# The order of the last three products of a down projection, and the width of its closing layer norm

## The chip, the cores and the metric

The kernel runs on one core of one Trainium2 chip. A time is device microseconds of one execution, from start to end; lower is better. The engines of a core work side by side, each through its own queue in order: PE (matrix multiply), DVE (elementwise and statistics), ACT (casts and activation functions), POOL and SP, which here mostly issue transfers. PE writes its results to banks of a small accumulator memory, from which DVE and ACT read them.

## The reference

The reference is one layer of a hybrid decoder on 1024 positions of 1024 columns in float32: layer norm, a gated mix of a convolution branch and a state-space branch, a projection, a layer norm, then a gated feed-forward block with a causal convolution, and a last layer norm. What the change touches is the end of it:

```python
def conv_ffn(h, w_up, dw_w, dw_b, w_down):
    u = causal_dwconv(h @ w_up, dw_w, dw_b)
    gate, val = jnp.split(u, 2, axis=-1)
    return (jax.nn.silu(gate) * val) @ w_down
...
        ffn = conv_ffn(h, w_ffn_up[l], ffn_dw_w[l], ffn_dw_b[l], w_ffn_down[l])
        h = layer_norm(DN_ALPHA * h + ffn, ln2_g[l], ln2_b[l])
```

The down projection multiplies 1024 x 2816 activations by a 2816 x 1024 weight matrix; the result is added to the residual rows times 2 to the power 1/4, and each row is normalised, scaled and shifted.

## The kernel before

**Precision.** Each float32 operand is split into a high part (a cast by ACT, L1192) and a low part (the operand minus the high part, by DVE, L1193). A block product is three matmuls: high by high (L180), high by low (L181), low by high (L182).

**The down projection** (`down`) is computed by a scheme of Strassen's kind. Rows, columns and the inner dimension are halved, and seven products of sums of quarters replace eight plain ones. The tuple `products` gives their order. A product has 11 steps (`k`); a step multiplies one 128-deep slice into four banks, one for each row tile of 128 rows by 512 columns, so a product has 11 x 4 x 3 = 132 matmuls. There are two sets of four banks: X (`acc` in the profile) and Y (`sm`). A product marked `True` starts its banks anew; one marked `False` adds to what is in them, which is how the sums of products are formed. The function named third in each entry runs for each row tile when the product is complete: DVE adds the bank to the rows (`own`, L1210, with the residual's factor; `more`, L1213, without) or subtracts it. Product numbers in the code run from 0; the text counts from the first to the seventh.

**Rows.** `rows` holds the eight output tiles (rs[0] to rs[7]) of 128 rows, each with an early half E and a late half L of 512 columns. The residual reaches them from memory by `load_rows`, on POOL's queue: one small copy, then four transfers of 256 KB. Row tiles 0 to 3 are complete after `four`, row tiles 4 to 7 after `three`. Each of these two takes the statistics of its half (L224) and calls `ln_out` for the tile: aggregate of the statistics (L238), square root on ACT (L239), reciprocal (L240), then the normalisation in two passes over the columns (L244: subtract the mean, times g; L247: times the reciprocal, plus b), and the store by SP.

**Loading.** `load` prepares one step: SP loads the activation slice, and a weight quarter or two, to tiles `dr` and `do` of 1024 columns that come from two pools of three; DVE adds two quarters where the product wants a sum (L1122); ACT casts; DVE subtracts. The result is a tile `w_dn`, from two pools of three that take turns, so a step's tile comes free when PE is done with the step six before. The last four steps of the last product have a tile of their own (`last`). In the fifth product (`five`) the weight is the sum of `a21` and `a22`: two weight loads and an addition for each step. In the sixth (`four`) it is `a22`: one load, no addition. In the seventh (`three`) it stands ready in `c4`.

**What sets the order.** The order on each engine is a scheduler's, which works from the order of the code and the priorities in it: loads have a high one (L1147), `ln_out` of tile 7 has a raised one, the other tiles' `ln_out` have none. In the seventh product the last eight steps run bank by bank, so that the banks are completed 24 matmuls apart; in the others all four banks are completed in the last step.

Of the kernel before, what the change touches and what calls it, by code (L numbers as in the profile page):

```python
# [17 lines left out]
D = 1024  # L18
T = 1024
HALF = 512  # L20
# [34 lines left out]
def kernel(  # L55
# [15 lines left out]
    V, A, G, TE, SY = nc.vector, nc.scalar, nc.gpsimd, nc.tensor, nc.sync  # L71
# [1013 lines left out]
    def down(upp, dp):  # L1085

        LAST, EARLY = 8, 5
        X, Y = [bank(1) for _ in range(4)], [bank(0) for _ in range(4)]  # L1090

        def flat_big(name):
            return big_tile(name).bitcast(F32).rearrange("p i k t -> p (i k t)")

        kept, rows = flat_big("c3"), flat_big("rows")
        c3 = [kept[:, k * HALF : (k + 1) * HALF] for k in range(NK)]
        c4 = [dp.tile([P, HALF], F32, name=f"c4_{k}") for k in range(NK - 1)]
        c4.append(upp.tile([P, HALF], F32, tag="s3", name="c4_last"))
        rs = [rows[:, t * D : (t + 1) * D] for t in range(8)]
        sts = [dp.tile([P, 2, 6], F32, name=f"st_f{t}") for t in range(8)]  # L1100

        E, L = slice(0, HALF), slice(HALF, D)
        gb = []

        def load_rows(p, w):
            t0, cs = {0: (0, E), 1: (0, L), 2: (4, L), 4: (4, E)}[p]
            G.tensor_copy(
                rows.rearrange("p (t n) -> p t n", n=D)[:, t0 : t0 + 4, cs.start : cs.start + 1],
                w[:, 0, :4].bitcast(F32).unsqueeze(2),
            )  # L1110
            for t in range(t0, t0 + 4):
                G.dma_start(rs[t][:, cs], h1_scr[t * P : (t + 1) * P, cs])
            if p == 2:
                dp.tile([P, 32], F32, name="down_pad")
                for n, start in (("g", RW_2G), ("b", RW_2B)):
                    r = upp.tile([P, D], F32, tag="o", bufs=3, name=f"ln2_{n}")
                    G.dma_start(r, prow[start : start + D].partition_broadcast(P))
                    gb.append(r)


        def add(dst, x, y):
            V.tensor_tensor(out=dst, in0=x, in1=y, op=ALU.add)  # L1122

        n_steps, n_raw = 0, 0

        def raw(name):
            nonlocal n_raw
            n_raw += 1
            pl, tag = ((wst, "st"), (upp, "raw"))[n_raw % 2]
            return pl.tile([P, D], F32, tag=tag, bufs=3, name=f"{name}_{n_raw}")  # L1130

        last = []

        def load(p, k):

            nonlocal n_steps
            a11, a21, a12, a22 = (wdown[h * NK + k, :, cs] for h in range(2) for cs in (E, L))
            x = (
                b11_scr[k],
                b2_scr[k][:, E],  # L1140
                t32_scr[k][:, L],
                t32_scr[k][:, E],
                t41_scr[k][:, L],
                t41_scr[k][:, E],
                b2_scr[k][:, L],
            )[p]
            with tc.high_priority(offset=4000):  # L1147
                st = raw("dr")
                w_st = st[:, E]
                SY.dma_start(st[:, L], x)  # L1150
                if p == 0 and k < EARLY:
                    SY.dma_start(w_st, a11)
                    G.tensor_copy(c3[k], w_st)
                elif p == 0:
                    w_st = c3[k]
                    SY.dma_start(w_st, a11)
                elif p == 1:
                    w_st = c4[k]
                    SY.dma_start(w_st, a12)
                elif p == 2:  # L1160
                    other = raw("do")[:, E]
                    SY.dma_start(other, a21)
                    SY.dma_start(w_st, a22)
                    add(c3[k], c3[k], other)
                    add(w_st, w_st, c3[k])
                    add(c4[k], c4[k], w_st)
                elif p == 3:
                    w_st = c3[k]
                elif p == 4:
                    other = raw("do")[:, E]  # L1170
                    SY.dma_start(w_st, a21)
                    SY.dma_start(other, a22)
                    add(w_st, w_st, other)
                elif p == 5:
                    SY.dma_start(w_st, a22)
                else:
                    w_st = c4[k]
                if p == 6 and k >= NK - 4:
                    if not last:
                        last.append(big_tile("last").rearrange("p i k t -> p (i k t)"))  # L1180
                    w = last[0][:, (k - NK + 4) * 2 * D : (k - NK + 5) * 2 * D]
                    w = w.rearrange("p (i n) -> p i n", i=2)
                else:
                    own = n_steps % 2 and n_steps > 2
                    w = (dp if own else wsp).tile(
                        [P, 2, D], F32R, tag="w", bufs=3, name=f"w_dn{p}_{k}"
                    )
                cuts = ((slice(0, D), st),) if w_st is not c3[k] and w_st is not c4[k] else (
                    (E, w_st), (L, st[:, L])
                )  # L1190
                for cs, src in cuts:
                    A.copy(w[:, 0, cs], src)  # L1192
                    V.tensor_tensor(  # L1193
                        out=w[:, 1, cs], in0=src, in1=w[:, 0, cs].bitcast(F32), op=ALU.subtract
                    )
            n_steps += 1
            return w

        def block(ps, w, t, first, k):
            mm3(  # L1200
                ps,
                lambda i: w[:, i, HALF + t * P : HALF + (t + 1) * P],
                lambda i: w[:, i, :HALF],
                first and k == 0,
                k == NK - 1,
                not first,
            )

        def own(ps, r, cs, op):
            V.scalar_tensor_tensor(out=r[:, cs], in0=r[:, cs], scalar=ALPHA, in1=ps, op0=ALU.mult, op1=op)  # L1210

        def more(ps, r, cs, op):
            V.tensor_tensor(out=r[:, cs], in0=r[:, cs], in1=ps, op=op)  # L1213

        def one(t):
            own(X[t], rs[t], E, ALU.add)

        def two(t):
            more(Y[t], rs[t], E, ALU.add)
            ln_part(dp, rs[t], sts[t], 0)  # L1220

        def six(t):
            own(X[t], rs[t], L, ALU.subtract)

        def seven(t):
            own(Y[t], rs[4 + t], L, ALU.add)

        def five(t):
            more(X[t], rs[4 + t], L, ALU.subtract)
            ln_part(dp, rs[4 + t], sts[4 + t], 1)  # L1230

        def four(t):
            more(Y[t], rs[t], L, ALU.add)
            ln_part(dp, rs[t], sts[t], 1)
            ln_out(dp, t, rs[t], *gb, sts[t])

        def three(t):
            own(X[t], rs[4 + t], E, ALU.add)
            ln_part(dp, rs[4 + t], sts[4 + t], 0)
            ln_out(dp, 4 + t, rs[4 + t], *gb, sts[4 + t])  # L1240

        products = (
            (X, True, one),
            (Y, True, two),
            (X, False, six),
            (Y, True, seven),
            (X, False, five),
            (Y, False, four),
            (X, False, three),
        )  # L1250
        for p, (banks, first, then) in enumerate(products):
            end = NK - LAST if p == 6 else NK
            for k in range(end):
                w = load(p, k)
                for t in range(4):
                    block(banks[t], w, t, first, k)
                if k == 4 and p in (0, 1, 2, 4):
                    load_rows(p, w)
            ws = {k: load(p, k) for k in range(end, NK)}
            for t in range(4):  # L1260
                for k in ws:
                    block(banks[t], ws[k], t, first, k)
                then(t)

    def ln_out(own, t, r, g, b, st):

        with tc.high_priority(offset=200 if t == 7 else 0):
            mv, rstd = ln_stats(own, [r], f"f{t}", [st])
            halves = [slice(q * HALF, (q + 1) * HALF) for q in range(2)]
            for cs in halves:  # L1270
                ln_apply(r[:, cs], mv, rstd, 0, g[:, cs], b[:, cs])
                SY.dma_start(out[t * P : (t + 1) * P, cs], r[:, cs])

# [143 lines left out]
```

## Time and profile before

| what | value |
|---|---|
| time, median of 3 runs | 1951.15 us (1951.04 to 1954.07) |
| the profiled execution, first to last instruction | 1951.6 us |
| PE busy | 1926.3 us (99%) |
| DVE busy | 1633.5 us (84%) |
| ACT busy | 1105.9 us (57%) |
| POOL busy | 133.7 us (7%) |
| fifth, sixth and seventh product start at | 1852.06, 1881.98 and 1911.90 us |
| last matmul ends at | 1941.98 us |

The profile's own execution has no time beside its span; the span is 0.45 us above the median of the runs. PE is the busiest engine. A row of the timeline reads: start, duration, engine, line of the code, operation, the tile written and the tiles read, size, and in brackets how long the engine had stood idle and what ended that. An instruction's duration is a little longer than the distance to the next one on a full engine, since the two overlap.

### The profile page before, as it was taken

To read this page: it belongs to the slowest core of one execution; us is meant where nothing else is said; L and a number is where in the kernel's file an instruction comes from. 1 tells how busy PE (TensorE), PEld (TensorE's weight loads), DVE (VectorE), ACT (ScalarE), POOL (GpSimd) and SP (SyncE) were. 2 spreads that over 40 slices of the span, in tenths; PEclk is the share of its full clock that TensorE was granted. 3 is DMA by queue.
4 is the path that set the end of the run, shared out by engine and by line. 5 is a ranking of instruction groups with operands and counts; after the bars stand their busy time and mean duration, and the time that the engine had idled before them with its cause. 6 is when DMAs were issued, how large, how long until landed. Compare 5 with 4: busy or idle time off the path is not lost.

```text
span 1951.6 us, 24929 instructions
## 1 busy us (share of the span) xinstructions
PE 1926.3 (99%) x9128; PEld 1575.7 (81%) x9128; DVE 1633.5 (84%) x2215; ACT 1105.9 (57%) x1841; POOL 133.7 (7%) x184
## 2 busy tenths in 40 slices
PE   7999999999999999999999999999999999999998
PEld 6888888887888887888888888888888888888886
DVE  7799999997666889999999956588998887878778
ACT  6767777664453367877765545365655454453442
POOL 0100000000400010000000040001000000011000
PEclk9999999999999999999999999999999999999999
DMA  6434343534546542424353454576443332368572
GB/s 223 132 114 130 108 136 118 177 100 141 178 128 215 207 131 96 143 104 136 107 174 108 139 180 129 159 267 243 156 157 108 113 103 90 113 230 268 180 253 108
DMA packets 104011, 297.68 MB, mean 153 GB/s; under 512 B 12432, under 2 KB 12464, under 8 KB 103888
## 3 DMA queue, kind: packets, MB, share of 16 engines
q1 hardware_dynamic: 87840, 244.68, 37.5%
q0 software_dynamic: 13744, 47.21, 7.8%
q10 hardware_dynamic: 2304, 4.20, 0.6%
q8 instruction: 71, 1.16, 0.3%
q14 instruction: 52, 0.43, 0.1%
HBM read 246.22 MB, written 49.82 MB: 152 GB/s over the span
## 4 chain that ended last, share of the span: by engine, by line
PE 78%; issue 11%; DVE 5%; DMA 3%; ACT 2%; POOL 1%; SPq 0%; DVEq 0%; ACTq 0%; POOLq 0%
PE acc L181 21%; PE acc L180 21%; PE acc L182 21%; PE sm L180 3%; PE sm L182 3%; PE sm L181 3%; PE sm L642 2%; PE sm L628 1%; PE sm L632 1%; DMA do<-wdown 1%; PE sm L593 1%; PE acc L333 1%; DMA m<-cum_scr 1%; DVE w_dn L1193 1%; DVE rows L244 1%
## 5 line engine op out<-in xcount | busy, mean ns | idle before, releaser
L545 DVE SCALAR_TENSOR_TENSOR c<-v,pc,c 128x512 f32<-128x512 f32 x480 | 346.1, 749 | 6.8 <-ACT c L534 5.6
L180 PE MATMUL acc<-hT,w_c 128*128 128x512 f32 x368 | 147.2, 400 | 0.0
L181 PE MATMUL acc<-hT,w_c 128*128 128x512 f32 x368 | 146.9, 399 | 0.0
L182 PE MATMUL acc<-hT,w_c 128*128 128x512 f32 x368 | 144.9, 394 | 0.0
L607 ACT ACTIVATE m<-m,cums 128x128 f32<-128x128 f32 x256 | 79.0, 398 | 64.5 <-DMA m<-cum_scr 60.7
L1052 DVE SCALAR_TENSOR_TENSOR fo<-u,pc,fo 128x1024 f32<-128x1024 f32 x88 | 111.3, 1289 | 0.0
L500 DVE SCALAR_TENSOR_TENSOR xbc<-u,pc,xbc 128x512 f32<-128x512 f32 x144 | 105.9, 751 | 1.1 <-ACT xbc L498 0.9
L180 PE MATMUL acc<-h1s,w_s 128*128 128x512 f32 x264 | 103.4, 392 | 0.2 <-ACT u L1036 0.2
L182 PE MATMUL acc<-h1s,w_s 128*128 128x512 f32 x264 | 103.0, 390 | 0.0
L182 PE MATMUL acc<-hT,w_z 128*128 128x512 f32 x256 | 102.8, 402 | 0.0
L181 PE MATMUL acc<-h1s,w_s 128*128 128x512 f32 x264 | 102.7, 389 | 0.0
L180 PE MATMUL acc<-hT,w_z 128*128 128x512 f32 x256 | 101.9, 398 | 0.4 <-ACT sig L521 0.4
L1192 ACT CAST w_dn<-dr 128x1024 fp32r<-128x1024 f32 (+1 forms) x73 | 60.7, 843 | 72.1 <-DVE dr L1122 42.5
L181 PE MATMUL acc<-hT,w_z 128*128 128x512 f32 x256 | 101.1, 395 | 0.0
L181 PEld LDWEIGHTS acc<-hT,w_c 128*128 128x128 f32 x368 | 69.2, 188 | 16.3 <-issue 3.1
L1193 DVE TENSOR_TENSOR w_dn<-dr,w_dn 128x1024 fp32r<-128x1024 f32 (+1 forms) x73 | 70.2, 971 | 13.8 <-ACT w_dn L1192 13.6
L182 PEld LDWEIGHTS acc<-hT,w_c 128*128 128x128 f32 x368 | 69.2, 188 | 15.6 <-issue 1.9
L180 PEld LDWEIGHTS acc<-hT,w_c 128*128 128x128 f32 x368 | 69.2, 188 | 15.5 <-issue 1.9
L147 DVE TENSOR_TENSOR w_c<-st_c,w_c 128x1024 fp32r<-128x1024 f32 x46 | 56.1, 1219 | 19.3 <-ACT w_c L146 19.3
L146 ACT CAST w_c<-st_c 128x1024 fp32r<-128x1024 f32 x46 | 48.3, 1051 | 40.7 <-PE acc L182 18.4
L180 PE MATMUL sm<-h1b,w_s 128*128 128x512 f32 x176 | 69.1, 393 | 0.0
L181 PE MATMUL sm<-h1b,w_s 128*128 128x512 f32 x176 | 69.0, 392 | 0.0
(382 smaller groups left out, 5596.2 us busy)
## 6 DMA issues: line engine op xcount, KB each, us to landing
st_c<-wcol SPq DMA_DIRECT2D x46, 512.0 KB, 3.5
st_z<-wz SPq DMA_DIRECT2D x32, 512.0 KB, 3.5
m<-cum_scr POOLq DMA_DIRECT2D x32, 512.0 KB, 4.7
st_wo<-wo SPq DMA_DIRECT2D x24, 512.0 KB, 4.1
ra<-wup SPq DMA_DIRECT2D x22, 512.0 KB, 3.8
rb<-wup SPq DMA_DIRECT2D x22, 512.0 KB, 3.3
t_scr<-fo POOLq DMA_DIRECT2D x22, 512.0 KB, 3.4
dr<-t_scr SPq DMA_DIRECT2D x44, 256.0 KB, 4.0
```

Source lines behind the costliest of these rows:

```text
L146: A.copy(w[:, 0, :], st)
L147: (eng or V).tensor_tensor(out=w[:, 1, :], in0=st, in1=w[:, 0, :].bitcast(F32), op=ALU.subtract)
L180: TE.matmul(ps, wa(0), xa(0), start=start, stop=False, skip_group_check=more)
L181: TE.matmul(ps, wa(0), xa(1), start=False, stop=False, skip_group_check=more)
L182: TE.matmul(ps, wa(1), xa(0), start=False, stop=stop, skip_group_check=more)
L500: V.scalar_tensor_tensor(out=o, in0=u[:, k : k + HALF], scalar=pc[:, wc + k : wc + k + 1], in1=o, op0=ALU.mult, op1=ALU.add,)
L545: V.scalar_tensor_tensor(out=accs[i], in0=v[:, k : k + HALF], scalar=pc[:, wc + k : wc + k + 1], in1=accs[i], op0=ALU.mult, op1=ALU.add,)
L607: A.activation(out=m[:, h, :], in_=m[:, h, :], func=AF.Relu, scale=-1.0, bias=cums[:, c, k : k + 1],)
L642: TE.matmul(py[h % 2 * HP : (h % 2 + 1) * HP, h // 2 * P : (h // 2 + 1) * P], xs[:, h * HP : (h + 1) * HP], m[:, h, :], start=True, stop=True,
L1052: V.scalar_tensor_tensor(out=o, in0=u[:, k : k + T], scalar=pc[:, wc + k : wc + k + 1], in1=o, op0=ALU.mult, op1=ALU.add,)
L1192: A.copy(w[:, 0, cs], src)
L1193: V.tensor_tensor(out=w[:, 1, cs], in0=src, in1=w[:, 0, cs].bitcast(F32), op=ALU.subtract)
```

## The change

Two things change. The fifth and the sixth product change places, with all that belongs to them: what is loaded and added, which banks they use, and which function runs behind them. As the banks stay with the functions, the order of the bank sets becomes X, Y, X, Y, Y, X, X in place of X, Y, X, Y, X, Y, X. The last load of residual rows moves with the product that has the two weight loads, from the fifth to the sixth. And `ln_out` works on all 1024 columns of a tile at once, with one store of 512 KB, except for tile 7, which keeps its two halves.

```diff
-            t0, cs = {0: (0, E), 1: (0, L), 2: (4, L), 4: (4, E)}[p]
+            t0, cs = {0: (0, E), 1: (0, L), 2: (4, L), 5: (4, E)}[p]
...
                 t32_scr[k][:, E],
+                t41_scr[k][:, E],
                 t41_scr[k][:, L],
-                t41_scr[k][:, E],
                 b2_scr[k][:, L],
             )[p]
...
                 elif p == 4:
+                    SY.dma_start(w_st, a22)
+                elif p == 5:
                     other = raw("do")[:, E]
                     SY.dma_start(w_st, a21)
                     SY.dma_start(other, a22)
                     add(w_st, w_st, other)
-                elif p == 5:
-                    SY.dma_start(w_st, a22)
...
             (Y, True, seven),
+            (Y, False, four),
             (X, False, five),
-            (Y, False, four),
             (X, False, three),
...
-                if k == 4 and p in (0, 1, 2, 4):
+                if k == 4 and p in (0, 1, 2, 5):
                     load_rows(p, w)
...
-            halves = [slice(q * HALF, (q + 1) * HALF) for q in range(2)]
-            for cs in halves:
+            for cs in (slice(0, HALF), slice(HALF, D)) if t == 7 else (slice(0, D),):
                 ln_apply(r[:, cs], mv, rstd, 0, g[:, cs], b[:, cs])
                 SY.dma_start(out[t * P : (t + 1) * P, cs], r[:, cs])
```

On PE, at the end of the sixth product and the start of the seventh, these rows stand before the change (`sm` and `acc` are banks, `w_dn_10` is the weight tile of step 10 of the sixth product, `w_dn_0` that of step 0 of the seventh):

```order
L180 MATMUL sm_13908<-w_dn_10_15294 128x512
L181 MATMUL sm_13908<-w_dn_10_15294 128x512
L182 MATMUL sm_13908<-w_dn_10_15294 128x512
L180 MATMUL acc_13901<-w_dn_0_15363 128x512
L181 MATMUL acc_13901<-w_dn_0_15363 128x512
L182 MATMUL acc_13901<-w_dn_0_15363 128x512
```

and these after it:

```order
L181 MATMUL acc_13903<-w_dn_10_15326 128x512
L182 MATMUL acc_13903<-w_dn_10_15326 128x512
L181 MATMUL acc_13904<-w_dn_10_15326 128x512
L182 MATMUL acc_13904<-w_dn_10_15326 128x512
L180 MATMUL acc_13901<-w_dn_0_15351 128x512
L181 MATMUL acc_13901<-w_dn_0_15351 128x512
```

The seventh product now begins in the banks in which the sixth has just ended; before, it began in the other set.

On DVE, around the first read of the sixth product's result, these rows stand before the change (the subtractions for the first steps of the seventh product, with the read of `sm_13905` among them):

```order
L1193 TENSOR_TENSOR w_dn_2_15401<-c_2_13913,w_dn_2_15401 128x512
L1193 TENSOR_TENSOR w_dn_2_15401<-dr_15399,w_dn_2_15401 128x512
L1193 TENSOR_TENSOR last<-dr_15446,last 128x512
L1193 TENSOR_TENSOR w_dn_3_15420<-c_3_13914,w_dn_3_15420 128x512
L1193 TENSOR_TENSOR w_dn_3_15420<-dr_15418,w_dn_3_15420 128x512
L1193 TENSOR_TENSOR last<-dr_15453,last 128x512
L1193 TENSOR_TENSOR last<-dr_15459,last 128x512
L1213 TENSOR_TENSOR rows<-rows,sm_13905 128x512
```

and these after it:

```order
L247 SCALAR_TENSOR_TENSOR rows<-rows,rs_f_15088,ln_b 128x1024
L1193 TENSOR_TENSOR w_dn_10_15326<-dr_15320,w_dn_10_15326 128x1024
L1193 TENSOR_TENSOR w_dn_1_15370<-c_1_13912,w_dn_1_15370 128x512
L247 SCALAR_TENSOR_TENSOR rows<-rows,rs_f_15098,ln_b 128x1024
L1193 TENSOR_TENSOR w_dn_1_15370<-dr_15368,w_dn_1_15370 128x512
L1193 TENSOR_TENSOR w_dn_2_15389<-c_2_13913,w_dn_2_15389 128x512
L1193 TENSOR_TENSOR w_dn_2_15389<-dr_15387,w_dn_2_15389 128x512
L1193 TENSOR_TENSOR w_dn_3_15408<-c_3_13914,w_dn_3_15408 128x512
L1193 TENSOR_TENSOR w_dn_3_15408<-dr_15406,w_dn_3_15408 128x512
L1193 TENSOR_TENSOR w_dn_4_15415<-c_4_13915,w_dn_4_15415 128x512
L1193 TENSOR_TENSOR w_dn_4_15415<-dr_15413,w_dn_4_15415 128x512
L1213 TENSOR_TENSOR rows<-rows,acc_13901 128x512
```

The normalisation of row tiles 0 to 3 (the last two L247 of it are seen here) now stands ahead of the first read of the sixth product's banks; before, it stood behind the reads, in the seventh product.

At DVE's end, these rows stand before the change, for row tiles 6 and 7 (`acc_13904` is the bank of tile 7; `st_f_13928` and `st_f_13929` are the statistics of the two):

```order
L244 SCALAR_TENSOR_TENSOR rows<-rows,mv_f_15571,ln_g 128x512 x2
L1210 SCALAR_TENSOR_TENSOR rows<-rows,acc_13904 128x512
L240 RECIPROCAL rs_f_15572<-rs_f_15572 128x1
L224 BN_STATS st_f_13929<-rows 128x6
L247 SCALAR_TENSOR_TENSOR rows<-rows,rs_f_15572,ln_b 128x512 x2
L238 BN_AGGR mv_f_15608<-st_f_13929 128x2
L244 SCALAR_TENSOR_TENSOR rows<-rows,mv_f_15608,ln_g 128x512 x2
L240 RECIPROCAL rs_f_15609<-rs_f_15609 128x1
L247 SCALAR_TENSOR_TENSOR rows<-rows,rs_f_15609,ln_b 128x512 x2
```

and these after it:

```order
L244 SCALAR_TENSOR_TENSOR rows<-rows,mv_f_15553,ln_g 128x1024
L240 RECIPROCAL rs_f_15554<-rs_f_15554 128x1
L247 SCALAR_TENSOR_TENSOR rows<-rows,rs_f_15554,ln_b 128x1024
L1210 SCALAR_TENSOR_TENSOR rows<-rows,acc_13904 128x512
L224 BN_STATS st_f_13929<-rows 128x6
L238 BN_AGGR mv_f_15587<-st_f_13929 128x2
L244 SCALAR_TENSOR_TENSOR rows<-rows,mv_f_15587,ln_g 128x512 x2
L240 RECIPROCAL rs_f_15588<-rs_f_15588 128x1
L247 SCALAR_TENSOR_TENSOR rows<-rows,rs_f_15588,ln_b 128x512 x2
```

Tile 6 is now finished ahead of the read of tile 7's bank; before, parts of it stood among the instructions of tile 7. On SP the stores of tiles 0 to 3 now stand among the loads for the seventh product; before, all sixteen stores stood behind the last load.

## The prediction

> **What bounds the kernel now.** I read the windows view first, cut at the borders of the products of the down projection: the third product ends at 1822.15, then come the fourth, fifth, sixth and seventh, and the last row is what follows the last matmul.
>
> ```profile
> core 0: us, PE busy (x) PEld busy (x) DVE busy (x) ACT busy (x) POOL busy (x), PEclk, DMA share, GB/s
> 1822.15:1852.06 29.91, 29.91 (x133) 24.78 (x132) 20.64 (x31) 13.09 (x21) 0.00 (x0) 1.00 0.59 187
> 1852.06:1881.98 29.92, 29.92 (x133) 24.78 (x132) 20.04 (x23) 11.62 (x12) 2.75 (x5) 1.00 0.85 294
> 1881.98:1911.90 29.92, 29.92 (x133) 24.78 (x132) 21.61 (x28) 14.28 (x20) 0.00 (x0) 1.00 0.53 168
> 1911.90:1941.98 30.08, 30.08 (x133) 24.59 (x131) 30.01 (x60) 6.05 (x13) 0.00 (x0) 1.00 0.28 106
> 1941.98:1951.60 9.62, 0.00 (x1) 0.00 (x0) 6.29 (x12) 0.29 (x1) 0.00 (x0) 0.69 0.28 110
> ```
>
> In all four products PE is busy for the whole stretch, at the full granted clock. A microsecond that PE waits here is a microsecond of the kernel, and work that leaves DVE inside a product is worth nothing. DVE has 8 to 10 us free in the fourth, fifth and sixth product and none in the seventh. Only the last 9.62 us belong to DVE and the stores. The timeline shows these, with the last matmul ahead and the matmul that starts each of two products behind:
>
> ```profile
> 1941.59 0.39 PE L182 MATMUL acc<-last 128*128 128x512 f32 x1
> 1940.23 0.69 DVE L224 BATCH_NORM_STATS2 st_f<-rows 128x6 f32<-128x512 f32 x1
> 1940.95 0.21 DVE L238 BATCH_NORM_AGGREGATE mv_f<-st_f 128x2 f32<-128x12 f32 x1
> 1941.20 1.42 DVE L244 SCALAR_TENSOR_TENSOR rows<-rows,mv_f,ln_g 128x512 f32<-128x512 f32 x2
> 1942.53 0.68 DVE L1210 SCALAR_TENSOR_TENSOR rows<-rows,acc 128x512 f32<-128x512 f32 x1
> 1943.13 0.16 DVE L240 RECIPROCAL rs_f<-rs_f 128x1 f32<-128x1 f32 x1
> 1943.24 0.69 DVE L224 BATCH_NORM_STATS2 st_f<-rows 128x6 f32<-128x512 f32 x1
> 1943.85 1.40 DVE L247 SCALAR_TENSOR_TENSOR rows<-rows,rs_f,ln_b 128x512 f32<-128x512 f32 x2
> 1945.17 0.20 DVE L238 BATCH_NORM_AGGREGATE mv_f<-st_f 128x2 f32<-128x12 f32 x1
> 1945.41 1.42 DVE L244 SCALAR_TENSOR_TENSOR rows<-rows,mv_f,ln_g 128x512 f32<-128x512 f32 x2
> 1946.74 0.16 DVE L240 RECIPROCAL rs_f<-rs_f 128x1 f32<-128x1 f32 x1
> 1946.93 1.41 DVE L247 SCALAR_TENSOR_TENSOR rows<-rows,rs_f,ln_b 128x512 f32<-128x512 f32 x2
> ...
> 1881.98 0.39 PE L180 MATMUL sm<-w_dn 128*128 128x512 f32 x1
> 1911.90 0.39 PE L180 MATMUL acc<-w_dn 128*128 128x512 f32 x1
> ```
>
> The last matmul ends at 1941.59 + 0.39 = 1941.98. Row tile 7 is read 0.55 us later, since DVE is still at tile 6, and between its statistics and its aggregate stand 1.3 us of tile 6 (L247, 1943.85). Its last application ends at 1948.34, 6.36 us after the last matmul; 3.26 us of store and end follow.
>
> **Term 1, the end: -1.8 us.** In the changed order the rows 0 to 3 are off DVE before the last product, so tile 6 (bank full 24 matmuls, 5.4 us, ahead of tile 7's) is through in about 4.4 us, before tile 7's bank is full. Tile 7 then runs alone: read 0.60 (1942.53 to 1943.13), statistics to aggregate 0.72 (1940.23 to 1940.95), to the first application 0.25 (to 1941.20), that pair 1.33 (1945.41 to 1946.74), to the second pair 0.19, and the pair 1.41: 4.50, with 0.05 from matmul to read 4.55. Against 6.36 that is 1.8 less. The stores of tile 7 stay two halves, as now, so I keep the 3.26 behind them.
>
> **Term 2, the two borders where a product now follows another in the same banks.** The fifth product adds into the `sm` banks that the fourth has just filled, the seventh into the `acc` banks of the sixth. PE must wait there until DVE has read the bank. Before, a whole product lay between.
>
> Fourth to fifth costs nothing: ahead of the first read DVE has only the subtraction of step 3, whose weight tile comes free six steps earlier, 5.4 us ahead of the border. With a cast of 1.05 (the row of 1850.55 below) and a subtraction of 1.22 it ends some 2.9 us ahead. The first bank is full 1.9 us ahead of the border (its third matmul starts ten matmuls of 29.92 / 132 = 0.227 ahead, and runs 0.39). The step-4 subtraction then lies between the first and the second read; the second ends some 0.65 us behind the border, and its bank is wanted at 0.68. Zero to 0.3 us; I take 0.
>
> Sixth to seventh is the costly one. Between the first read of an `sm` bank (`four`) and the first read of an `acc` bank (`five`), inclusive, the changed DVE order has 47 instructions: 5 reads, 4 statistics, 5 additions of `a21` and `a22` and 10 subtractions of 512 columns, 7 subtractions of 1024, 8 applications of 1024, 8 aggregates and reciprocals. Their pitch, from one start to the next on a full DVE:
>
> ```profile
> 1883.59 1.22 DVE L1193 TENSOR_TENSOR w_dn<-dr,w_dn 128x1024 fp32r<-128x1024 f32 x1
> 1884.72 0.68 DVE L1213 TENSOR_TENSOR rows<-rows,acc 128x512 f32<-128x512 f32 x1
> 1885.32 0.68 DVE L224 BATCH_NORM_STATS2 st_f<-rows 128x6 f32<-128x512 f32 x1
> 1885.92 1.26 DVE L1213 TENSOR_TENSOR rows<-rows,acc 128x512 f32<-128x512 f32 x2
> ...
> 1696.44 1.28 DVE L1052 SCALAR_TENSOR_TENSOR fo<-u,pc,fo 128x1024 f32<-128x1024 f32 x1
> 1697.63 1.22 DVE L884 TENSOR_TENSOR w_s<-rb,w_s 128x1024 fp32r<-128x1024 f32 x1
> ...
> 1921.90 0.16 DVE L240 RECIPROCAL rs_f<-rs_f 128x1 f32<-128x1 f32 x1
> 1921.97 1.39 DVE L244 SCALAR_TENSOR_TENSOR rows<-rows,mv_f,ln_g 128x512 f32<-128x512 f32 x2
> ```
>
> 512 columns: 0.60 (1884.72, 1885.32, 1885.92). A subtraction of 1024: 1.13. An application of 1024 columns does not occur yet; the same operation at that width is L1052, 1.19. The small ones: 0.07 to 0.11, say 0.09. Sum: 24 x 0.60 = 14.4, 7 x 1.13 = 7.9, 8 x 1.19 = 9.5, 8 x 0.09 = 0.7, together 32.5 us, in a product of 29.92. DVE goes over by 2.6 us, and all of it lies ahead of the read that PE waits for. The width alone saves 0.14 each (a pair of halves takes 1.33, above), 1.1 us in the eight.
>
> When does this run of work start, and where does DVE idle in it? The nearest rows are the fifth product of now, which has the same two loads and one addition per step that the sixth is to have:
>
> ```profile
> 1852.06 0.39 PE L180 MATMUL acc<-w_dn 128*128 128x512 f32 x1
> 1854.41 0.68 DVE L1210 SCALAR_TENSOR_TENSOR rows<-rows,sm 128x512 f32<-128x512 f32 x1
> ...
> 1859.18 0.69 DVE L1122 TENSOR_TENSOR dr<-dr,do 128x512 f32<-128x512 f32 x1 [1.16 <-DMA dr<-wdown]
> ...
> 1864.29 0.69 DVE L1122 TENSOR_TENSOR dr<-dr,do 128x512 f32<-128x512 f32 x1 [1.94 <-DMA dr<-wdown]
> ...
> 1850.55 1.05 ACT L1192 CAST w_dn<-dr 128x1024 fp32r<-128x1024 f32 x1 [5.39 <-DVE dr L1122]
> ...
> 1839.20 1.66 ACT L1192 CAST last<-c 128x512 fp32r<-128x512 f32 x3 [2.12 <-DVE w_dn L1193]
> 1840.77 0.62 ACT L1192 CAST last<-c_last 128x512 fp32r<-128x512 f32 x1
> ```
>
> There the first read came 2.35 us behind the border, since it stands behind additions that wait for loads. It cannot come before the bank is full, 1.9 us ahead. Between -1.9 and +2.35 I take +0.7: nearer to the row, and 1.65 earlier because the four casts of `last` (2.1 us on ACT), which delayed the first weights of now's fifth product, lie a product further back for the sixth. For idle time inside, the two waits shown make 3.1 us, the upper end; 0 is the lower. I take 0.7, since 12 us of norm work now stand between the loads' users. So the read that PE waits for ends at 0.7 + 32.5 + 0.7 + 0.1 = 34.0 behind the border of the sixth product, PE wants it at 29.9, and starts again 0.1 later: **a stall of 4.2 us**, most of it in one gap.
>
> **What is hidden.** Four square roots and the table load move among ACT's casts: ACT has 29.92 - 14.28 = 15.6 us free there. The four stores of rows 0 to 3 now stand in SP's queue among the loads of the seventh product and wait for their applications; the loads behind them feed subtractions that stand behind the same applications on DVE. Were that cover gone, it would cost one landing:
>
> ```profile
> dr<-b_scr SPq DMA_DIRECT2D x11, 256.0 KB, 2.7
> rows<-h_scr POOLq DMA_DIRECT2D x4, 256.0 KB, 6.5
> ```
>
> POOL's copy and its four loads (6.5 us to landing) go from the fifth product to the sixth with the two-load steps that they disturb already. They are needed a product later. Behind the stall DVE has 3 more reads, 4 weight subtractions, 4 of `last` and 4 statistics, 9 us, before the weights of step 6 are due, 53 matmuls or 12 us behind the restart: no second stall.
>
> **Sum.** -1.8 + 0 + 4.2 = +2.4 us. The profiled span, 1951.6, would be 1954.0; it lies 0.45 above the median of the runs, 1951.15, to which I add the same 2.4: **1953.6**. A measurement of this kernel tells about 0.2% from no change, 3.9 us.
>
> **Bounds.** First read at -1.9 and no idling: stall 0.9, net -0.9, 1950.2. First read at +2.35: net +4.0, 1955.2. Idling of 3.1: net +4.8, 1956.0. Both together: +6.4, 1957.6.
>
> **Rival on the slower side: the clock falls in the gap.** After the last matmul the granted clock did this:
>
> ```profile
> 1945.40:1945.60 0.20, 0.00 (x0) 0.00 (x0) 0.19 (x1) 0.20 (x1) 0.00 (x0) 1.00 0.67 266
> 1945.60:1945.80 0.20, 0.00 (x0) 0.00 (x0) 0.20 (x1) 0.10 (x1) 0.00 (x0) 0.54 1.13 440
> ```
>
> It fell to half some 3.6 us after PE stopped. A stall over 3.6 us can reach that, and 4.2 is over it, though by little; one row does not say how the point varies. No row shows the way back. If it takes 3.6 us of work again, those run at half rate and 1.8 us are lost: net +4.2, 1955.4, slower. The bounds are 0 and the whole last product at half rate, 30 us, which I leave out. I give 0.18. [...]
>
> **Other rivals.** DVE keeps up: loads are ready early, as one load per step in the new fifth product would allow; stall under 2.5, net -0.9 to +0.7, about 1951: 0.17. Against it speaks 32.5 over 29.9. Loads late and the first read late, net above +4, about 1957: 0.08, slower. The end doesn't get shorter because tile 6 still stands in the way: term 1 gone, 1955.4, slower: 0.02. Nothing reaches faster: term 1 alone is 1.8, half of what could be told; I leave 0.02 for what the profile doesn't show.
>
> **Chances.** The forecast, net +0.7 to +3.9, has 0.53. Within 0.2%: 0.53 + 0.17 = 0.70. Slower: 0.18 + 0.08 + 0.02 = 0.28. Faster: 0.02. The range 1950.2 to 1957.0 reaches from the lower bound over the clock rival to near both upper bounds together.
>
> **What would show it.** One PE wait at the first matmul of the seventh product, on L1213 (`five`), of 4 us, and none at the start of the fifth; DVE full through the sixth product; 4.5 us from the last matmul to the end of the last application. No such wait, or one spread over the additions in the sixth product, proves the sum of DVE's work or its start wrong; a granted clock under 1.00 behind the wait proves the rival.

## The result and the profile after

The changed kernel is slower. Its six runs have a median of 1957.82 us (1956.32 to 1960.36), the kernel before on the same chip 1952.19 (1951.04 to 1954.07): 5.6 us more, ratio 1.0029 with a 95% interval of [1.0018, 1.0041]. The profiled execution took 1958.34 us, 1956.6 of it span, against a span of 1951.6.

The windows view of the changed kernel, cut at its own borders: fourth, fifth and sixth product, what lies between sixth and seventh, the seventh, and what follows the last matmul.

```profile
core 0: us, PE busy (x) PEld busy (x) DVE busy (x) ACT busy (x) POOL busy (x), PEclk, DMA share, GB/s
1822.99:1852.91 29.92, 29.92 (x133) 24.77 (x132) 20.19 (x29) 14.20 (x21) 0.00 (x0) 1.00 0.60 200
1852.91:1882.83 29.92, 29.92 (x133) 24.77 (x132) 16.87 (x18) 11.57 (x11) 0.83 (x3) 1.00 0.58 185
1882.83:1912.75 29.92, 29.92 (x133) 24.59 (x131) 29.11 (x42) 14.08 (x21) 1.52 (x3) 1.00 0.81 273
1912.75:1916.82 4.07, 0.17 (x1) 0.00 (x0) 4.07 (x8) 1.76 (x3) 0.00 (x0) 1.00 0.86 285
1916.82:1948.66 31.84, 31.83 (x132) 25.85 (x132) 21.54 (x33) 3.89 (x8) 0.00 (x0) 0.95 0.13 50
1948.66:1956.60 7.94, 0.00 (x0) 0.00 (x0) 4.50 (x8) 0.29 (x1) 0.00 (x0) 0.71 0.31 122
```

Three things differ from before: a stretch of 4.07 us in which PE is done and DVE is full, a seventh product of 31.84 in place of 30.08 at a mean clock of 0.95, and an end of 7.94 in place of 9.62. DVE, free for 8 us in the sixth product before, is now full there. From 1700 us to the end of the span the view of PE's waits has a single row (us in total, times, longest):

```profile
PE acc L180 <- DVE rows L1213: 3.9, 1, 3.9
```

The timeline shows the run of DVE's work that PE waits for, and PE on both sides of the gap:

```profile
1883.63 0.69 DVE L1122 TENSOR_TENSOR dr<-dr,do 128x512 f32<-128x512 f32 x1 [2.08 <-issue]
1884.24 0.68 DVE L1213 TENSOR_TENSOR rows<-rows,sm 128x512 f32<-128x512 f32 x1
...
1916.09 2.47 DVE L1213 TENSOR_TENSOR rows<-rows,acc 128x512 f32<-128x512 f32 x4
...
1912.53 0.39 PE L182 MATMUL acc<-w_dn 128*128 128x512 f32 x1
1916.82 0.50 PE L180 MATMUL acc<-w_dn 128*128 128x512 f32 x1 [3.91 <-DVE rows L1213]
```

The first `sm` read comes 1884.24 - 1882.83 = 1.41 us behind the border of the sixth product, 31.85 later the first `acc` read, and 0.7 later PE starts: 4.29 us between two matmuls in place of 0.23, so 4.06 lost.

Behind the gap the windows of one microsecond show the granted clock (the column after the five engines, 1.00 being full):

```profile
1916.00:1917.00 1.00, 0.18 (x1) 0.18 (x2) 1.00 (x3) 0.62 (x1) 0.00 (x0) 1.00 0.69 231
1917.00:1918.00 1.00, 1.00 (x5) 0.82 (x6) 1.00 (x3) 0.62 (x1) 0.00 (x0) 0.96 0.82 268
1918.00:1919.00 1.00, 1.00 (x4) 0.79 (x3) 1.00 (x2) 0.63 (x1) 0.00 (x0) 0.50 0.41 148
...
1921.00:1922.00 1.00, 1.00 (x5) 0.78 (x5) 1.00 (x2) 0.00 (x0) 0.00 (x0) 0.84 0.00 0
1922.00:1923.00 1.00, 1.00 (x6) 0.82 (x5) 1.00 (x3) 0.00 (x0) 0.00 (x0) 1.00 0.00 0
```

It stands at one half for 3.4 us, from 1917.9 to 1921.3, with PE back at work. From its first to its last matmul the seventh product takes 31.45 us, where before it took 29.69: 1.76 lost. The end, from the timeline:

```profile
1946.34 1.28 DVE L247 SCALAR_TENSOR_TENSOR rows<-rows,rs_f,ln_b 128x1024 f32<-128x1024 f32 x1
1948.69 0.69 DVE L1210 SCALAR_TENSOR_TENSOR rows<-rows,acc 128x512 f32<-128x512 f32 x1 [1.06 <-PE acc L182]
...
1951.92 1.41 DVE L247 SCALAR_TENSOR_TENSOR rows<-rows,rs_f,ln_b 128x512 f32<-128x512 f32 x2
...
1948.27 0.39 PE L182 MATMUL acc<-last 128*128 128x512 f32 x1
```

Tile 6 is through before tile 7's bank is full (DVE waits 1.06 us for PE), and the last application ends 1953.33 - 1948.66 = 4.67 behind the last matmul.

The sum for the profiled pair: 4.06 + 1.76 - 1.68 = +4.14 from the sixth product on. The other 0.85 of the 5.0 lies ahead of it: the sixth product starts at 1882.83 in place of 1881.98.

### The profile page after: what moved, and what is told of

The parts are those of the page before. It is cut to its first block, busy times and chain, and to the rows that moved or that the text cites. A ratio compares the mean times of both kernels' runs of the same rounds, so it can differ in the third digit from the quotient of the medians.

```text
span 1956.6 us, 24899 instructions
## 1 busy us (share of the span) xinstructions
PE 1926.6 (98%) x9128; PEld 1576.3 (81%) x9128; DVE 1632.2 (83%) x2201; ACT 1106.0 (57%) x1841; POOL 134.8 (7%) x184
## 4 chain that ended last, share of the span: by engine, by line
PE 80%; issue 11%; DVE 4%; DMA 2%; ACT 2%; POOL 1%; SPq 0%; DVEq 0%; POOLq 0%; ACTq 0%
PE acc L181 21%; PE acc L180 21%; PE acc L182 21%; PE sm L181 3%; PE sm L182 3%; PE sm L180 3%; PE sm L642 2%; PE sm L628 1%; PE sm L632 1%; PE sm L593 1%; DVE w_dn L1193 1%; DMA m<-cum_scr 1%; DMA st_wo<-wo 1%; PE acc L333 1%; POOL var L781 0%
```

## The experiments

The numbers below stand in one table, to which the text comes back. All are worked out from the timelines as above: how far the first `sm` read lies behind the start of the sixth product; from it to the first `acc` read; what the sixth product takes from its first to its last matmul beyond 29.69 (PE's waits, and in order_only a slow clock too); PE's extra time between sixth and seventh (in filled and filled6 with the matmuls that were put there); the seventh product from first to last matmul; the end behind the last matmul. The ratio is to the kernel before on the same chip, with its 95% interval.

| kernel | first `sm` read | to first `acc` read | inside sixth | border | seventh | end | ratio |
|---|---|---|---|---|---|---|---|
| before | - | - | 0 | 0 | 29.69 | 9.62 | 1 |
| changed | +1.41 | 31.85 | 0 | 4.06 | 31.45 | 7.94 | 1.0029 [1.0018, 1.0041] |
| after_again | +4.18 | 32.31 | 2.66 | 4.65 | 32.68 | 7.91 | 1.0035 [1.0022, 1.0047] |
| order_only | +3.89 | 33.64 | 4.22 | 4.12 | 31.42 | 7.95 | 1.0038 [1.0025, 1.005] |
| wide_only | - | - | 0 | 0 | 29.69 | 7.97 | 0.9993 [0.9984, 1.0001] |
| filled | +2.15 | 32.03 | 0.34 | 4.66 | 29.83 | 7.94 | 1.0027 [1.0017, 1.0036] |
| filled6 | +2.91 | 31.85 | 0.90 | 4.66 | 31.46 | 7.97 | (one run) |
| one_load | -0.62 | 32.58 | 0 | 2.78 | 29.83 | 7.58 | 1.001 [1.0001, 1.0019] |
| held23 | +2.25 | 33.61 | 0 | 6.77 | 32.02 | 9.61 | 1.0047 [1.0033, 1.006] |
| gate2 | +2.37 | 28.24 | 0.38 | 1.03 | 29.81 | 10.92 | 1.0015 [1.0006, 1.0024] |
| gate1 | +2.14 | 27.03 | 0.13 | 0 | 29.98 | 11.30 | 1.0014 [1.0005, 1.0023] |
| g24 | +2.37 | 28.24 | 0.38 | 1.03 | 29.81 | 9.07 | 1.0002 [0.9993, 1.0011] |
| add_pool | +0.05 | 36.42 | 3.52 | 3.85 | 32.54 | 9.02 | 1.0033 [1.002, 1.0046] |
| g24_pool | -0.91 | 32.00 | 0.54 | 1.46 | 34.88 | 9.01 | 1.0036 [1.0024, 1.0049] |

### The two halves of the change, each alone

order_only keeps the order of the change and has every application in two halves:

```
-            for cs in (slice(0, HALF), slice(HALF, D)) if t == 7 else (slice(0, D),):
+            halves = [slice(q * HALF, (q + 1) * HALF) for q in range(2)]
+            for cs in halves:
```

> The order of the products as changed, all norm applications in two halves of 512 columns as before. Theory (the cost is the work that DVE has ahead of the first read of the `acc` banks, and then the clock that falls in the gap): eight more instructions, 1.0 us more on DVE, so a wait of PE at the first matmul of the seventh product of 5.1 us (4.06 in the changed kernel), the granted clock falls behind it as there, 1.7 us lost; against the kernel before +6 us, 1.0 more than the changed kernel. Rival (the wide applications cost something by themselves, for example by later stores): the time comes out below that of the changed kernel.

wide_only keeps the order of before (`four` sixth, its two-load steps and its row loads in the fifth product) and has the wide applications.

> The order of the products as before, the applications 1024 columns wide but for row tile 7. Theory: no product follows another in the same banks, so no wait at a border and a full clock to the last matmul; tile 6 is off DVE some 0.1 to 0.3 us sooner at the end (0.14 for each pair), so -0.3 to 0 us against the kernel before: the same. Rival (the width is what costs): +1 us or more.

Order alone costs as much as the whole change: 1.0038 against 1.0029 and 1.0035, with 33.64 us from read to read where the wide kernel has 31.9 to 32.3. The expected 1.0 us between them is below what the intervals can tell. The wait at the border is 4.12 in place of the expected 5.1, because a part of the loss came earlier: inside the sixth product PE waited 2.04 us for weights, and the granted clock fell to one half behind that wait already, 10 us before it fell again in the seventh product.

```profile
1910.08 0.50 PE L181 MATMUL acc<-w_dn 128*128 128x512 f32 x1 [2.04 <-DVE w_dn L1193]
```

```profile
1911.00:1912.00 1.00, 1.00 (x5) 0.77 (x4) 1.00 (x3) 0.57 (x2) 0.00 (x0) 0.56 0.74 215
...
1914.00:1915.00 1.00, 1.00 (x4) 0.73 (x4) 1.00 (x3) 0.93 (x2) 0.00 (x0) 0.73 0.75 217
```

The width alone costs nothing, and the end gains more by it than the 0.3 us that I expected at most. From its timeline:

```profile
1940.98 1.28 DVE L247 SCALAR_TENSOR_TENSOR rows<-rows,rs_f,ln_b 128x1024 f32<-128x1024 f32 x1
1942.18 0.68 DVE L1210 SCALAR_TENSOR_TENSOR rows<-rows,acc 128x512 f32<-128x512 f32 x1
...
1945.39 1.42 DVE L247 SCALAR_TENSOR_TENSOR rows<-rows,rs_f,ln_b 128x512 f32<-128x512 f32 x2
```

With the last matmul at 1942.13, tile 6 is through at once behind it and tile 7 is read at 1942.18; the end is 7.97, as short as with the new order. I had counted 0.14 us for one tile's pair, but before this edit DVE is full through the seventh product, so what is saved in all seven tiles, by estimate 14 pairs at 0.14 or 2.0 us, reaches the end. In the profiles either half of the change alone takes the 1.7 us; together they take them once. What the order adds is loss only.

### Is the slow stretch the clock?

filled puts 15 matmuls into the gap, of weights that are there, into an `sm` bank that nobody reads any more:

```
+            if p == 6:
+                for _ in range(15):
+                    TE.matmul(Y[0], w[:, 1, HALF : HALF + P], w[:, 0, :HALF], start=True, stop=True)
```

> The changed kernel with 15 matmuls more ahead of the seventh product: weights that are there already, times one another, into an `sm` bank that nobody reads any more (3.4 us of the gap of 4.3). They wait for nothing of DVE, and the product behind them starts when DVE has read the bank, as before. Theory (the slow stretch behind the gap is the clock, which falls because PE is idle): the wait left is under 1 us, the granted clock stays 1.00 and the matmuls of the seventh product run at 0.227 us from the first one: 1.7 us below the changed kernel, +3.3 against the kernel before in the profiled span. Rival (what is slow behind the gap is something else, for example the stores and loads at that place): the first 3 us of the seventh product are as slow as in the changed kernel, and the time is the same.

Its timeline and two windows:

```profile
1912.68 3.56 PE L1255 MATMUL sm<-w_dn 128*128 128x512 f32 x15
1917.34 0.50 PE L180 MATMUL acc<-w_dn 128*128 128x512 f32 x1 [1.10 <-DVE rows L1213]
```

```profile
1917.00:1918.00 1.00, 0.66 (x3) 0.57 (x4) 1.00 (x3) 0.68 (x2) 0.00 (x0) 1.00 0.78 242
1918.00:1919.00 1.00, 1.00 (x6) 0.82 (x5) 1.00 (x3) 0.49 (x2) 0.00 (x0) 1.00 0.81 264
```

DVE, the loads and the stores do at that place what they do in the changed kernel, PE only isn't idle, and the clock stays at 1.00: the seventh product takes 29.83 in place of 31.45. So the 1.6 us are the clock's. In the medians they can't be told (1.0027 against 1.0029 and 1.0035): the run of DVE's work started 0.7 us later in this profile than in the first one of the changed kernel, and between the changed kernel's own two profiles its start differs by more than 1.6 (table).

filled6, with 6 matmuls in place of 15, was to show how short a pause is enough.

> As filled, with 6 matmuls in place of 15: PE runs 1.4 us into the gap and then stands for some 3 us. If the granted clock falls only when PE stands for longer than the 3.6 us at which it fell behind the last matmul of the kernel before, it stays 1.00 and the seventh product takes 29.8 us; if a shorter pause is enough, it falls as in the changed kernel and the product takes 31.4.

```profile
1914.92 1.52 PE L1255 MATMUL sm<-w_dn 128*128 128x512 f32 x6
1919.58 0.73 PE L180 MATMUL acc<-w_dn 128*128 128x512 f32 x1 [3.14 <-DVE rows L1213]
```

```profile
1920.00:1921.00 1.00, 1.00 (x4) 0.71 (x4) 1.00 (x3) 1.00 (x3) 0.00 (x0) 0.50 0.69 207
```

PE was idle for 3.14 us and the product behind it took 31.46: the clock fell. A pause shorter than 3.6 us was enough.

### The changed kernel again

> The changed kernel once more, beside the others on the same chip. Theory: the wait at the first matmul of the seventh product is there in every run, 4.0 us give or take 0.5, and the clock falls behind it; the work ahead of the fourth product, which is the same in both kernels, ends within 1 us of where it ends before, in either direction. Rival (part of the difference comes from the work ahead, which the change is not supposed to touch): the fourth product starts 0.8 us or more later again.

Median 1960.25 us of five runs against 1953.04: +7.2, and the profile is not the first one over again. The fourth product starts at 1821.25, earlier than in both first profiles (1822.99 in the changed kernel, 1822.14 before), so the work ahead does not explain the slower time. Over all profiles of this record, whose code ahead of it is the same, that start lies anywhere from 1819.74 (gate1) to 1824.26 (filled6), more than most effects here; so the sums count from the sixth product on. The wait is 4.65, above the expected 4.0 give or take 0.5. What differs is the start of DVE's run. Timeline, and the rows of PE's waits:

```profile
1884.66 0.69 DVE L1122 TENSOR_TENSOR dr<-dr,do 128x512 f32<-128x512 f32 x1 [3.51 <-issue]
1885.27 0.68 DVE L1213 TENSOR_TENSOR rows<-rows,sm 128x512 f32<-128x512 f32 x1
...
1917.58 2.47 DVE L1213 TENSOR_TENSOR rows<-rows,acc 128x512 f32<-128x512 f32 x4
```

```profile
PE acc L180 <- DVE rows L1213: 4.5, 1, 4.5
PE acc L181 <- DVE w_dn L1193: 2.2, 3, 1.5
```

The sixth product starts at 1881.09, so the first `sm` read is 4.18 us late, not 1.41. It stands on DVE behind an addition of `a21` and `a22`. The work behind it takes nearly the same time, so all of it is some 2.8 later, and now even the weights of the sixth product's last steps come late: 2.66 us of waits inside the product, then 4.65 at the border. The clock stays at one half for 6.8 us:

```profile
1917.00:1918.00 1.00, 0.00 (x0) 0.00 (x0) 1.00 (x3) 0.24 (x1) 0.00 (x0) 0.80 0.78 266
1918.00:1919.00 1.00, 0.68 (x2) 0.59 (x3) 1.00 (x3) 0.85 (x2) 0.00 (x0) 0.50 0.75 266
...
1923.00:1924.00 1.00, 1.00 (x3) 0.74 (x3) 1.00 (x3) 0.00 (x0) 0.00 (x0) 0.50 0.00 0
1924.00:1925.00 1.00, 1.00 (x5) 0.79 (x4) 1.00 (x3) 0.00 (x0) 0.00 (x0) 0.79 0.00 0
```

That costs 32.68 - 29.69 = 2.99. Sum against before: 2.66 + 4.65 + 2.99 - 1.71 = 8.6, less 0.9 by which the sixth product started earlier: 7.7, the difference of the spans (1959.3 - 1951.6).

### What makes the start late

one_load takes one load out of each step of the sixth product and leaves DVE's instructions as they are (it multiplies by 2 x `a21`):

```
-                    other = raw("do")[:, E]
+                    raw("do")
                     SY.dma_start(w_st, a21)
-                    SY.dma_start(other, a22)
-                    add(w_st, w_st, other)
+                    add(w_st, w_st, w_st)
```

> The changed kernel, but the sixth product uses 2 x `a21` in place of `a21` + `a22`: one load of 256 KB less in each of its steps, with every addition and every other instruction of DVE as in the changed kernel (the output is wrong by that). Theory (the first `sm` read is late by the loads: it stands behind an addition that waits for `a22`, by 1.4, 4.2 and in the other variants 2.1 to 3.9 us behind the border): the first `sm` read comes within 0.5 us of the border, the 47 instructions still take 32 to 33 us, the wait of PE is 2 to 3 us in place of 4.1 and 4.5, and no wait is left inside the sixth product; where the wait stays under 3.6 us the clock stays 1.00. Together 2.5 to 5 us below the changed kernel, +0.5 to +3 against the kernel before. Rival (the lateness comes from DVE itself): first read and wait as in the changed kernel, and the same time.

```profile
1880.77 0.69 DVE L1122 TENSOR_TENSOR dr<-dr 128x512 f32<-128x512 f32 x1 [1.35 <-DMA dr<-wdown]
1881.38 0.68 DVE L1212 TENSOR_TENSOR rows<-rows,sm 128x512 f32<-128x512 f32 x1
...
1913.96 2.47 DVE L1212 TENSOR_TENSOR rows<-rows,acc 128x512 f32<-128x512 f32 x4
...
1914.70 0.50 PE L180 MATMUL acc<-w_dn 128*128 128x512 f32 x1 [2.61 <-DVE rows L1212]
```

```profile
1914.00:1915.00 1.00, 0.30 (x1) 0.30 (x2) 1.00 (x3) 0.75 (x2) 0.00 (x0) 1.00 0.88 207
```

The sixth product starts at 1882.00; the first `sm` read now comes 0.62 ahead of that, the work takes 32.58, the wait is 2.78, nothing is lost inside the product, and with 2.6 us of idle PE the clock stays at 1.00 in this profile (in order_only it fell behind a wait of 2.04). The ratio is 1.001, 2.0 us in the medians: about a third of the changed kernel's loss. So the run of work alone, with its start undisturbed, gives a wait of 2.8 us; the lateness of the loads gives the rest, and with it the longer pause behind which the clock fell in both profiles of the changed kernel. Which load is late stays open: in the changed kernel's rows the idle time ahead of the addition ends with "issue", not with a transfer, and one_load also has less to transfer altogether.

add_pool tried to take the additions off DVE:

```
-                    add(w_st, w_st, other)
+                    G.tensor_tensor(out=w_st, in0=w_st, in1=other, op=ALU.add)
```

> The changed kernel with the additions of `a21` and `a22` of the sixth product on POOL in place of DVE (1.6 us each there, by POOL's additions of 128x512 elsewhere in the kernel, one for each step of 2.7 us). Theory (the first `acc` read comes at its start plus the work in between, and its start, the first `sm` read, is late because it stands behind an addition that waits for its loads): without additions on DVE the first `sm` read no longer waits for loads and comes within 0.7 us of the border of the sixth product (+1.4 and +4.2 in the two profiles of the changed kernel); of the work 28.4 us are left, less 0.6 to 1.2 for what the order shifts; the wait of PE falls under 1 us, the clock stays 1.00, and the time is 5 to 7 us below the changed kernel. Rival (the loads come late whatever engine adds, so PE waits for the weights inside the sixth product instead): the wait moves there, and the time stays within 2 us of the changed kernel.

The first `sm` read is on time (+0.05), as expected, but the rest went the rival's way. The rows of PE's waits:

```profile
PE acc L180 <- DVE rows L1213: 3.7, 1, 3.7
PE acc L180 <- ACT w_dn L1192: 1.8, 1, 1.8
PE acc L181 <- DVE w_dn L1193: 1.1, 1, 1.1
```

POOL waits for the loads in DVE's place, the casts behind it are late, and DVE, with less to do, stands in its queue behind subtractions that wait for them: 36.42 us from read to read. The late transfer stopped the engine that came first in order: DVE in the changed kernel, POOL here.

### Less work ahead of the read

held23 holds the norm of row tiles 2 and 3 until the `acc` banks have been read, by a copy of one element from that read into the tile of statistics.

> The changed kernel, but the norm of row tiles 2 and 3 waits until the seventh product has begun: its statistics and applications are held behind the reads of the `acc` banks. Theory: ahead of the first read of `acc` DVE has 38 instructions, 26.8 us where the changed kernel has 32.5, less than a product's 29.9; the wait is under 1 us, the granted clock stays 1.00, the end stays as short as in the changed kernel as long as tiles 2 and 3 are through before the last matmul: -1.5 us against the kernel before, 5 to 6.5 below the changed kernel. Rival (loads of the two-load steps are late and bind instead): PE waits at borders of steps in the sixth or seventh product, and the time stays within 2 us of the changed kernel.

The theory failed. The scheduler filled the place with three subtractions of `last`, which wait for casts on ACT, and the read stands behind them:

```profile
1912.76 0.69 DVE L1193 TENSOR_TENSOR last<-dr,last 128x512 fp32r<-128x512 f32 x1 [2.53 <-ACT last L1192]
...
1916.74 0.69 DVE L1193 TENSOR_TENSOR last<-dr,last 128x512 fp32r<-128x512 f32 x1 [1.48 <-ACT last L1192]
1917.35 0.68 DVE L1213 TENSOR_TENSOR rows<-rows,acc 128x512 f32<-128x512 f32 x1
```

38 instructions took 33.61 us, 6.9 of it waiting (for a load, and for casts), and the wait at the border grew to 6.77. What matters is what stands ahead of the read and whether it can run, not how much norm there is.

The gate kernels therefore act on the order itself. Ten subtractions of the seventh product's weights stand ahead of the read in the changed kernel; most are not needed yet:

```
+                if p == 6 and k >= 2:
+                    gate = rs[7 if k >= NK - 4 else 4]
+                    V.tensor_copy(out=w[:, 1, ::HALF], in_=gate[:, HALF : HALF + 2])
```

> The changed kernel, and the second halves of the weights (the subtractions) of steps 2 to 10 of the seventh product wait for the reads of the `acc` banks, by a copy of two elements each. In the changed kernel ten such subtractions of 512 columns stand ahead of the first read of `acc`; here four do, and the `last` ones stay behind the reads too. Theory (what counts is what stands on DVE ahead of the read, whatever it is): 6 x 0.60 = 3.6 us less ahead of it, a wait of 0.5 us where the changed kernel has 4.06, the clock stays 1.00; the subtractions of step 2 are through 5.3 us behind the first read, wanted 5.4 us behind the restart, so no second wait; 5.2 us below the changed kernel. Rival (the waiting work only comes later): the steps behind the border are late by the same amount, and the time stays within 1.5 us of the changed kernel.

gate1 has `k >= 1`:

> As gate2, but from step 1 on: only step 0 of the seventh product is subtracted ahead of the first read. Theory: 4.8 us less ahead of the read, no wait at the border; but the subtractions of step 1 now end 5.3 us behind the first read, and PE wants them 2.7 us behind its start: a wait of about 1 us there, of the weights, too short for the clock to fall; in sum within 1 us of gate2. Rival (as for gate2): within 1.5 us of the changed kernel.

From the timeline and the windows of gate2:

```profile
1911.06 1.27 DVE L1216 TENSOR_TENSOR rows<-rows,acc 128x512 f32<-128x512 f32 x2
```

```profile
1941.98:1952.90 10.92, 0.00 (x0) 0.00 (x0) 7.55 (x13) 0.59 (x2) 0.00 (x0) 0.64 0.36 145
```

The work between the reads falls to 28.24 and 27.03, by 3.6 and 4.8 against the 31.85 of the changed kernel's first profile, as counted, and the wait at the border to 1.03 and 0; the wait for the weights of step 1 that was expected of gate1 did not come, and the clock stays. Some two thirds of the gain are given back at the end (10.9 and 11.3 us in place of 7.9): the scheduler reordered PE's last matmuls, and the tiles come closer together (2.95 us apart in gate2) than DVE can norm them (3.8 us each there). That gate2's median is still 5.2 us below the changed kernel's (1955.04 against 1960.25), as expected, is luck in part: the longer end was not in the expectation, nor were the +7.2 of the changed kernel in that set of runs. g24 gates steps 2 to 4 alone:

> As gate2, but only the subtractions of steps 2 to 4 of the seventh product are held behind the read of `acc`, and `last` is left alone. In gate2 the order of PE's last matmuls changed with it, so that the four row tiles end 2.95 us apart and DVE's norm of each takes 3.8: the end grew to 10.9 us behind the last matmul. Here tile 7's last 22 matmuls run alone, 5.0 us, tile 6's 16. Theory: a wait of 0.5 to 1.5 us at the border, no fall of the clock, an end of 8 to 9 us: 2 us below gate2, 0 to -1 against the kernel before. Rival: the end is as long as in gate2, and the time stays with it.

Ratio 1.0002: with a wait of 1.03, no fall of the clock and an end of 9.07 the change is back at the time of before (in its profile 1.0 us above it from the sixth product on). The last try joined it with add_pool:

> g24 and add_pool together. Theory: no wait at the border at all, no fall of the clock, an end of 8 to 9 us: -1 to -1.8 against the kernel before, the fastest of these. Rival (as for add_pool): weights late inside the sixth product, +2 us or more against the kernel before.

It is as slow as add_pool: 1.0036 [1.0024, 1.0049]. But the weights were late inside the sixth product by 0.24 us only, and the wait at the border is 1.46. The loss came one bank later: after the first `acc` read DVE was idle for 3.81 us, waiting for the cast that a subtraction of `last` needs; the second `acc` read stood behind that subtraction, PE was idle for 3.15 us, and the clock fell once more.

```profile
1917.47 0.69 DVE L1195 TENSOR_TENSOR last<-dr,last 128x512 fp32r<-128x512 f32 x1 [3.81 <-ACT last L1194]
...
1918.82 0.50 PE L180 MATMUL acc<-w_dn 128*128 128x512 f32 x1 [3.15 <-DVE rows L1215]
```

No version is told apart from the kernel before on the faster side; wide_only comes nearest.

## Why the prediction was wrong

**The clock rival.** This step failed most plainly. The text put the fall at 3.6 us after PE stops, the stall at 4.2, found it over "though by little", and gave it 0.18, leaving 1.8 us out of the sum. By its own two numbers it was the likelier case. Nor is 3.6 us a threshold: in the changed kernel's first profile the fall came 5.0 us after PE had stopped at the border (1917.9 against 1912.9) and 3.4 us after its last matmul (1952.04 against 1948.66). Inside the kernel it came in both profiles of the changed kernel and behind every wait of 3.1 us or more; it also came behind one of 2.04 us (order_only), and not behind one of 2.61 (one_load). In the changed kernel it cost 1.76 and 2.99 us; 1.8 was for a slow stretch of 3.6 us, and the one in after_again took 6.8. With it the forecast would have been 1955.4, still short of 1957.82.

**The start of DVE's run.** "Between -1.9 and +2.35 I take +0.7" took one row of before as the upper end. The runs show +1.41 and +4.18 for the changed kernel, and +2.1 to +3.9 in those variants that keep its loads and additions on DVE. The +0.7 was argued from the casts of `last`; the load that the addition waits for was named and not priced. This is the term that was mis-sized, and beyond its bound it brings a cost that the prediction did not have: 2.66 us inside the sixth product.

**The work and the wait.** 47 instructions at 32.5 us: 32.45 in the first profile (31.85 and a read of 0.60). Stall 4.2: 4.06. The second agreement is partly luck, since the start was 0.7 later than taken and the idle time 0.7 less.

**The other border** costs nothing, as predicted.

**The end.** -1.8 predicted, -1.68 measured, 4.67 us in place of 4.55 from matmul to last application. But the reason was only one of two: rows 0 to 3 need not leave the last product, the width alone does it. What the width saves was counted only in the eight applications ahead of the stall; "work that leaves DVE inside a product is worth nothing" does not hold for the seventh product, in which DVE was full.

**The sum.** For the profiled pair the wait and the end were right and the clock was missing: +2.4 forecast, +4.14 from the sixth product on, 0.85 more ahead of it. For the medians (+5.6 and +7.2) the late start comes on top, as after_again's profile and one_load suggest: the rival of late loads, given 0.08, was true at the same time as that of the clock. The two are not separate cases; the later the start, the longer the pause (+1.41 and 4.06 in the changed kernel's first profile, +4.18 and 4.65 in after_again's). And 1.04 us of the distance from 1953.6 to 1957.82 is the base alone: the forecast was added to the median of three runs, 1951.15, and with six it is 1952.19.

## What to carry to other kernels

When a product is moved so that it adds to banks that must first be read, count what stands in the reading engine's queue ahead of the read and whether each of it can run: one late load there was a wait of the matrix engine, whichever engine added (2.66 us inside the sixth product in after_again, where DVE adds, 3.52 in add_pool, where POOL does). Price a pause of TensorE with the clock behind it (here the clock fell behind one of 2.04 us, and the changed kernel lost 1.76 and 2.99 us to it), as part of the sum and not as a rival, and take a load's lateness from several rows, not one. Before crediting an edit with a gain at the end, ask whether the other half of the change gives it alone.

## What the runs showed of the hardware

With PE back at work, the clock's low stretches came in two lengths, each worked out from finer windows of the same view: 3.4 us in the changed kernel, order_only (twice), filled6 and g24_pool, 6.8 in after_again, held23 and add_pool. In order_only the clock falls at 1911.13, rises at 1914.54, falls again at 1921.37 and rises at 1924.78, both times 3.41 us behind the fall. In the three longer stretches PE was still idle when the clock fell: of their first 3.4 us it was busy for 1.28, 2.44 and 2.69 (held23, add_pool, after_again); in the shorter ones it was busy all the time.

The length of the pause alone did not decide whether the clock fell: one of 3.14 us (filled6) and one of 2.04 (order_only) were enough, one of 2.61 (one_load) was not; in the changed kernel the fall came 1.1 us after PE had started again. What else decides was not shown.

An addition of 128x512 in place took 1.30 us on POOL in add_pool (the median of 11), its rows on DVE 0.69.
